# Attention in a two-layer decoder trunk: filling products four steps ahead, queries split over all rows and placed by transfers, weight splits half a chunk ahead and in pieces

## The chip, the cores and the metric

The kernel runs on one core of a Trainium2 chip. The metric is the device time of one execution in microseconds (us): three executions gave 931.06, 931.27 and 932.01, the median is 931.27. One more execution was taken with the hardware profiler; all rows with start times come from it. The engines of a core are PE (TensorE, matrix products, with PEld for its weight loads), DVE (VectorE), ACT (ScalarE), POOL (GpSimd) and SP (SyncE, which here only issues DMA transfers). Each runs its own instructions in order and waits for others by semaphores.

## The reference

Two layers over a sequence of 512 tokens with 1024 features. Layer 0 mixes tokens by causal pooling, layer 1 by attention; a gated MLP follows each, with a norm ahead of every part. The change touches only the attention of layer 1:

```python
qkv = h @ w_qkv + b_qkv                    # 16 query heads, 4 key/value heads of 64
kb, vb = band(k), band(v)                  # this block of 128 keys and the one before
scores = einsum("bnqkgd,bnskd->bnkgqs", q, kb) * 64 ** -0.5
scores = where(mask, scores - slope * dist, -inf)      # window of 128, ALiBi
m = maximum(max(scores), sink)
p = exp(scores - m)
probs = p / (sum(p) + exp(sink - m))
o = einsum("bnkgqs,bnskd->bnqkgd", probs, vb)
h = h + o @ w_o
```

## The kernel before, in words

**Products of float32.** A float32 number is held as a rounded high part (`_h`) and the rest (`_l`). `mm3` (L82 to L86) makes a product of three: wh·xh (L84), wh·xl (L85), wl·xh (L86). So every operand is split: a cast to the high part and a subtraction for the low part. "A product" below is one of the three matmuls, "a step" one call of `mm3` over 512 columns.

**Weights.** `fetch` (L88 to L91) has SP issue the transfer of 128x1024 numbers (512 KB) into a `raw` tile, of which there are 3. `weights` (L93 to L100) casts it on ACT (L98) and subtracts on DVE or POOL (L99), into rings of 4 `wh` and 4 `wl` tiles. A fetch waits until the split of the weight three earlier has read its `raw` tile, a cast until PE has done with the weight four earlier.

**Attention, set-up** (L382 to L493). Ten chunks of 128 output columns hold keys (`kq0`, `kq1`) and queries (`kq2` to `kq9`, called query chunks 0 to 7); a chunk is 8 steps. Keys, values and the first two query chunks are made ahead of the main loop. `keys(n)` (L440) splits 64 rows of a key head and puts the same into the other 64 rows (ACT L449, DVE L450). `queries(c)` (L453) multiplies the chunk by the norm's factor (DVE L456), scales it and adds the bias (ACT L457), and for each of its two heads casts 64 rows (ACT L463) and subtracts into the other 64 rows (DVE L464); a tile `q` thus has a head's high part in one half of the rows and its low part in the other.

**Main loop** (L601 to L620). There are 16 units: four key heads n by four blocks b of 128 queries. Unit i runs `scores` (8 matmuls L548 into a PSUM bank, masked and reduced by DVE L551, POOL L562, exp on ACT L565, sums on DVE L567 and L568, normalised by POOL L570). In the same turn, unit i−3 runs `weighted` (6 or 12 products with the values, then ACT L597 and DVE L598 split the result into `oh` and `ol`), and unit i−2 runs `transposed` (4 or 8 transposes on PE, L578, split by ACT L581 and DVE L582 into `th` and `tl`). Key heads n+1 are placed in the block b = 2 of head n.

**Filling products.** PE would idle between these. `work()` (L509) is one list of steps to fill with: 48 steps of query chunks 2 to 7, then steps of the output projection with weights `wo0` to `wo3`, each with the number of units that must be done ahead of it. `fill(upto, have)` takes steps up to a number, as long as their need is met. In turn i the loop takes 2/3 of `RATE` = 4 steps after the scores and the rest after the transposes, up to step 4i + 4. At the head of a new key head it takes at least the steps that the head's query chunks need. After the loop the rest is taken, then `wo0` to `wo7` are finished (L622 to L627).

The order of the code sets the work around the change; the framework (`tile.TileContext`, L767) then gives each engine a sequence of its own, close to the code's but not equal to it, in which SP's fetches and transfers stand about where their buffers or data are ready.

Of the kernel before, what the change touches and what calls it, by code (L numbers as in the profile page):

```python
# [19 lines left out]
F32 = mybir.dt.float32  # L20
F32R = mybir.dt.float32r
# [5 lines left out]
P = 128  # L27
# [30 lines left out]
def trunk(ctx: ExitStack, tc: tile.TileContext, x_tok, x_t, vecs, w_pool, w_kq, w_v, w_o, w_in, w_out, out_a, out_b):  # L58
# [10 lines left out]
    def small(pool, n, words, dt=F32, **kw):  # L69
        return pool.tile([P, words], dt, **kw)[:, :n]  # L70
# [19 lines left out]
        nc.sync.dma_start(raw[:, :n], src)  # L90
        return raw  # L91

    def weights(src, n, name, eng=None, raw=None):  # L93

        raw = raw or fetch(src, n, name)
        h = wp.tile([P, 1024], F32R, tag="wh", name=f"{name}_h")
        l = wp.tile([P, 1024], F32R, tag="wl", name=f"{name}_l")
        A.activation(h[:, :n], raw[:, :n], AF.Copy)  # L98
        (eng or V).tensor_tensor(l[:, :n], raw[:, :n], h[:, :n].bitcast(F32), ALU.subtract)  # L99
        return h, l  # L100

    def part(w, k, m=P):
# [280 lines left out]
    with tc.tile_pool(name="ap", bufs=2) as ap:  # L383
# [20 lines left out]
        nsink = small(ap, NH, 64, name="nsink", bufs=1)  # L404
        V.tensor_scalar(nsink, vec[:, V_SINK : V_SINK + NH], -1.0, None, ALU.mult)

        def proj(i, ps, ks=range(NC), w=None):
            w = w or weights(w_kq[i], D, f"kq{i}", G if i > 3 else V)
            for k in ks:
                mm3(ps, part(w, k), xs1[k], k == 0, k == NC - 1)  # L410
            return w
# [28 lines left out]
        def keys(n):  # L440

            src = slice((n % 2) * HD, (n % 2 + 1) * HD)
            dst = slice((1 - n % 2) * HD, (2 - n % 2) * HD)
            u = ku[n // 2]
            kh = ap.tile([P, S], F32R, tag="kh", name=f"kh{n}")
            kl = ap.tile([P, S], F32R, tag="kl", name=f"kl{n}")
            A.activation(kh[src], u[src], AF.Copy)
            V.tensor_tensor(kl[src], u[src], kh[src].bitcast(F32), ALU.subtract)
            A.activation(kh[dst], u[src], AF.Copy)  # L449
            V.tensor_copy(kl[dst], kl[src].bitcast(F32))  # L450
            return kh, kl

        def queries(c, ps):  # L453

            u = sm.tile([P, S], F32, tag="sq", name=f"q{c}_u")
            V.tensor_tensor(u, ps, rb, ALU.mult)  # L456
            A.activation(u, u, AF.Identity, scale=qs[:, c : c + 1], bias=bqs[:, c : c + 1])  # L457
            res = []
            for par in range(2):
                src = slice(par * HD, (par + 1) * HD)  # L460
                dst = slice((1 - par) * HD, (2 - par) * HD)
                t = ap.tile([P, S], F32R, tag="q", name=f"q{c}_{par}", bufs=8)
                A.activation(t[src], u[src], AF.Copy)  # L463
                V.tensor_tensor(t[dst], u[src], t[src].bitcast(F32), ALU.subtract)  # L464
                res.append(t)
            return res

# [1 line left out]
        q = {0: queries(0, qps)}  # L469
        qps = bank("pj")  # L470
        proj(3, qps)
        for j in range(NT):
            ps = vps[j // 2][:, (j % 2) * 256 : (j % 2 + 1) * 256]
            vv = ap.tile([P, 256], F32, tag="vv", name=f"vv{j}", bufs=1)
            V.scalar_tensor_tensor(vv, ps, r[:, j : j + 1], vec[:, V_BV : V_BV + 256], ALU.mult, ALU.add)
            dh, dl = (t[:, j, : 8 * HD].rearrange("p (n z d) -> p n z d", n=4, z=2)[:, :, 1, :] for t in (vh, vl))
            v4 = vv.rearrange("p (n d) -> p n d", n=4)
            A.activation(dh, v4, AF.Copy)
            V.tensor_tensor(dl, v4, dh.bitcast(F32), ALU.subtract)
# [7 lines left out]
        def fill_q(c):  # L487
            st = {}
            for k in range(NC):
                if k == 0:  # L490
                    st["ps"] = bank("pj")
                    st["w"] = None
                st["w"] = proj(2 + c, st["ps"], [k], st["w"])  # L493
                if k == NC - 1:
                    q[c] = queries(c, st["ps"])
                yield
# [5 lines left out]

        def fill_wo(m, tag, ks):
            if m not in wo_w:
                wo_w[m] = weights(w_o[m], D, f"wo{m}", G if m < 4 else V)
                wo_ps[m] = bank(tag)
            yield from wo_steps(m, ks)

# [19 lines left out]
        def fill(upto, have):  # L528
            while done[0] < upto and need[0] <= have:
                need[0] = next(todo, 100)  # L530
                done[0] += 1

        def scores(n, b):
            w = P if b == 0 else 2 * P
            neg = small(ap, 4, 32, tag="neg", name=f"neg{n}{b}", bufs=3)
            den = small(ap, 4, 16, tag="den", name=f"den{n}{b}", bufs=3)
            es = small(ap, 4, 16, tag="es", name=f"es{n}{b}", bufs=3)
            sink = nsink[:, 4 * n : 4 * n + 4]
            kk = max(b - 1, 0) * P
            sc = []  # L540
            for pr in range(2):
                ps = bank("s")
                st = ap.tile([P, 2, 2 * P], F32, tag="sc", name=f"sc{n}{b}{pr}", bufs=6)
                for par in range(2):
                    o = ps[:, par * 256 : par * 256 + 256]
                    qt = q[2 * n + pr][par][:, b * P : (b + 1) * P]
                    for x, kt in enumerate(key[n]):
                        T.matmul(o, lhsT=qt, rhs=kt[:, kk : kk + 256], start=x == 0, stop=x == 1)  # L548
                for par in range(2):
                    i = 2 * pr + par  # L550
                    V.tensor_tensor_reduce(  # L551
                        out=st[:, par, :w],
                        in0=ps[:, par * 256 : par * 256 + w],
                        in1=dist[:, 2 * P - w :],
                        scale=-slopes[4 * n + i],
                        scalar=sink[:, i : i + 1],
                        op0=ALU.add,
                        op1=ALU.min,
                        accum_out=neg[:, i : i + 1],
                    )  # L560
                sc.append(st)
            G.tensor_tensor(es, neg, sink, ALU.subtract)  # L562
            heads = [sc[i // 2][:, i % 2, :w] for i in range(4)]
            for i, t in enumerate(heads):
                A.activation(t, t, AF.Exp, bias=neg[:, i : i + 1], scale=-1.0, accum_out=den[:, i : i + 1])  # L565
            A.activation(es, es, AF.Exp)
            V.tensor_tensor(den, den, es, ALU.add)  # L567
            V.reciprocal(den, den)  # L568
            for i, t in enumerate(heads):
                G.tensor_scalar(t, t, den[:, i : i + 1], 1.0, ALU.mult, ALU.mult)  # L570
            return sc
# [26 lines left out]
            V.tensor_tensor(dl, p2, dh.bitcast(F32), ALU.subtract)  # L598


        RATE = 4  # L601
        sc, pt = {}, {}
        for i in range(NU + 3):
            base = i * RATE
            have = max(i - 3, 0) if i < NU else NU
            if i < NU:
                n, b = units[i]
# [164 lines left out]
```

## Time and profile before

| what | value |
|---|---|
| median of three executions | 931.27 us |
| the profiled execution | 932.39 us |
| its span, first to last instruction | 930.6 us |
| mean granted PE clock | 0.996 of full speed |
| data moved by DMA | 88.13 MB, 95 GB/s |

Columns of the timeline: start, duration, engine, line, operation, output<-inputs, shape, count; in brackets the idle time ahead of it and what ended it. Matmuls overlap, so the distance between starts tells what one costs, rather than its duration. A row of the waits has the waiting engine and line, what it waited for, then us in total, times, and the longest. A row of the groups has count, busy us, mean ns of one, idle us ahead.

### The profile page before, as it was taken

To read this page: it belongs to the slowest core of one execution; us is meant where nothing else is said; L and a number is where in the kernel's file an instruction comes from. 1 tells how busy PE (TensorE), PEld (TensorE's weight loads), DVE (VectorE), ACT (ScalarE), POOL (GpSimd) and SP (SyncE) were. 2 spreads that over 40 slices of the span, in tenths; PEclk is the share of its full clock that TensorE was granted. 3 is DMA by queue.
4 is the path that set the end of the run, shared out by engine and by line. 5 is a ranking of instruction groups with operands and counts; after the bars stand their busy time and mean duration, and the time that the engine had idled before them with its cause. 6 is when DMAs were issued, how large, how long until landed. Compare 5 with 4: busy or idle time off the path is not lost.

```text
span 930.6 us, 11682 instructions
## 1 busy us (share of the span) xinstructions
PE 915.2 (98%) x4419; PEld 771.5 (83%) x4419; DVE 574.8 (62%) x945; ACT 427.3 (46%) x690; POOL 135.1 (15%) x217
## 2 busy tenths in 40 slices
PE   8999999999999999999899999999999999999996
PEld 7788888888888888898788888888888888888896
DVE  5679766335777754456777482987743377777433
ACT  7655443223444443337787451644422244444532
POOL 9600000000000001325654140000000000000022
PEclk9999999999999999999999999999999999999999
DMA  9133222333223223322111041242233422322312
GB/s 333 67 113 113 93 84 80 93 128 113 91 91 105 65 87 106 114 91 68 50 43 46 2 158 39 98 139 104 63 93 100 136 91 91 111 80 63 95 60 91
DMA packets 28855, 88.13 MB, mean 95 GB/s; under 512 B 3200, under 2 KB 4352, under 8 KB 28800
## 3 DMA queue, kind: packets, MB, share of 16 engines
q1 hardware_dynamic: 28800, 87.40, 28.5%
q8 instruction: 34, 0.56, 0.2%
q14 instruction: 21, 0.17, 0.1%
HBM read 85.29 MB, written 2.10 MB: 94 GB/s over the span
## 4 chain that ended last, share of the span: by engine, by line
PE 92%; ACT 3%; DVE 2%; POOL 2%; issue 1%; POOLq 0%; ACTq 0%
PE bank L84 30%; PE bank L85 30%; PE bank L86 30%; PE bank L548 1%; PE bank L578 1%; ACT sc L565 1%; DVE q L464 1%; ACT px_h L251 0%; POOL sc L570 0%; PE bank L241 0%; ACT q_u L457 0%; DVE sc L551 0%; ACT wi_h L98 0%; PE bank L271 0%; ACT th L581 0%
## 5 line engine op out<-in xcount | busy, mean ns | idle before, releaser
L224 POOL TENSOR_TENSOR n_acc<-n_acc,n_sq 128x512 f32<-128x512 f32 (+1 forms) x28 | 39.1, 1395 | 716.4 <-ACT n_sq L215 709.8
L98 ACT ACTIVATE wi_h<-wi_raw 128x1024 fp32r<-128x1024 f32 x88 | 93.0, 1061 | 109.0 <-PE bank L85 100.5
L85 PE MATMUL bank<-f0x_l,wi_h 128*128 128x512 f32 x352 | 137.1, 389 | 0.8 <-DVE f0x_l L252 0.8
L84 PE MATMUL bank<-f0x_h,wi_h 128*128 128x512 f32 x352 | 137.3, 390 | 0.0
L84 PE MATMUL bank<-f1x_h,wi_h 128*128 128x512 f32 x352 | 137.2, 390 | 0.0
L84 PE MATMUL bank<-zh,wo_h 128*128 128x512 f32 (+1 forms) x363 | 137.1, 378 | 0.0
L86 PE MATMUL bank<-f0x_h,wi_l 128*128 128x512 f32 x352 | 137.0, 389 | 0.0
L86 PE MATMUL bank<-f1x_h,wi_l 128*128 128x512 f32 x352 | 137.0, 389 | 0.0
L85 PE MATMUL bank<-f1x_l,wi_h 128*128 128x512 f32 x352 | 137.0, 389 | 0.0
L86 PE MATMUL bank<-zh,wo_l 128*128 128x512 f32 (+1 forms) x363 | 136.6, 376 | 0.0
L85 PE MATMUL bank<-zl,wo_h 128*128 128x512 f32 (+1 forms) x363 | 136.6, 376 | 0.0
L99 DVE TENSOR_TENSOR wi_l<-wi_raw,wi_h 128x1024 fp32r<-128x1024 f32 x84 | 102.6, 1223 | 49.2 <-ACT wi_h L98 37.3
L98 ACT ACTIVATE wo_h<-wo_raw 128x768 fp32r<-128x768 f32 (+1 forms) x70 | 57.5, 823 | 120.2 <-PE bank L85 108.5
L313 DVE TENSOR_TENSOR c_u<-bank,n_rb 128x512 f32<-128x512 f32 x88 | 59.9, 687 | 75.9 <-PE bank L86 75.9
L99 DVE TENSOR_TENSOR wo_l<-wo_raw,wo_h 128x768 fp32r<-128x768 f32 (+1 forms) x66 | 60.3, 914 | 54.4 <-ACT wo_h L98 54.2
L86 PEld LDWEIGHTS bank<-zh,wo_l 128*128 128x128 f32 x363 | 68.3, 188 | 12.5
L84 PEld LDWEIGHTS bank<-zh,wo_h 128*128 128x128 f32 x363 | 68.3, 188 | 12.3
L85 PEld LDWEIGHTS bank<-zl,wo_h 128*128 128x128 f32 x363 | 68.3, 188 | 12.3
L85 PEld LDWEIGHTS bank<-f0x_l,wi_h 128*128 128x128 f32 x352 | 66.1, 188 | 14.6 <-DVE f0x_l L252 1.2
L84 PEld LDWEIGHTS bank<-f0x_h,wi_h 128*128 128x128 f32 x352 | 66.1, 188 | 14.2 <-DVE h L305 0.4
L86 PEld LDWEIGHTS bank<-f1x_h,wi_l 128*128 128x128 f32 x352 | 66.1, 188 | 13.9
L316 ACT ACTIVATE c_t<-c_u,vec 128x512 f32<-128x512 f32 x88 | 70.6, 811 | 15.3 <-DVE c_u L313 14.5
(173 smaller groups left out, 1488.7 us busy)
## 6 DMA issues: line engine op xcount, KB each, us to landing
wi_raw<-w_in SPq DMA_DIRECT2D x88, 512.0 KB, 3.2
wo_raw<-w_out SPq DMA_DIRECT2D x31, 384.0 KB, 3.0
wo_raw<-w_out SPq DMA_DIRECT2D x31, 320.0 KB, 2.8
kq_raw<-w_kq SPq DMA_DIRECT2D x10, 512.0 KB, 3.2
wo_raw<-w_o SPq DMA_DIRECT2D x8, 512.0 KB, 3.2
xt<-x_tok SPq DMA_DIRECT2D x4, 512.0 KB, 5.2
h<-x_t SPq DMA_DIRECT2D x8, 256.0 KB, 7.5
wpool_raw<-w_pool SPq DMA_DIRECT2D x2, 512.0 KB, 8.5
```

Of the source, the lines that this page charges most:

```text
L84: T.matmul(ps, lhsT=wh, rhs=xh, start=start, stop=False, **kw)
L85: T.matmul(ps, lhsT=wh, rhs=xl, start=False, stop=False, **kw)
L86: T.matmul(ps, lhsT=wl, rhs=xh, start=False, stop=stop, **kw)
L98: A.activation(h[:, :n], raw[:, :n], AF.Copy)
L99: (eng or V).tensor_tensor(l[:, :n], raw[:, :n], h[:, :n].bitcast(F32), ALU.subtract)
L224: eng.tensor_tensor(self.acc[:, lo:hi], self.acc[:, lo:hi], sq[:, lo:hi], ALU.add)
L313: V.tensor_tensor(u, ps, rb, ALU.mult)
L316: A.activation(t, u, AF.Identity, bias=col(V_CB + layer * 2 * NF + m), scale=cw[2])
L464: V.tensor_tensor(t[dst], u[src], t[src].bitcast(F32), ALU.subtract)
L548: T.matmul(o, lhsT=qt, rhs=kt[:, kk : kk + 256], start=x == 0, stop=x == 1)
L565: A.activation(t, t, AF.Exp, bias=neg[:, i : i + 1], scale=-1.0, accum_out=den[:, i : i + 1])
L578: T.transpose(ps[:, i * P : (i + 1) * P], sc[i // 2][:, i % 2, kb * P : (kb + 1) * P], ident)
```

## The change

- `AHEAD` = 4: four filling steps are taken ahead of the first unit, and every limit in the loop is four steps higher.
- A query chunk is split over all 128 rows at once: one cast into a tile `qh`, one subtraction in place. The halves are then put into the `q` tiles by four transfers (`move`, each 64x512 numbers, 128 KB), issued by SP.
- The copies of the keys into the other 64 rows become two such transfers.
- The weights of a query chunk are asked for half a chunk ahead (at k = 4 of the chunk before) and not at its first step. From `kq5` on their subtraction is on POOL in four pieces of 256 columns, as is that of `wo0` to `wo3`; that of `kq4` moves from POOL to DVE.
- `vv` uses the ring `sc`, and `neg`, `den` and `es` have 2 buffers where they had 3.

```diff
-    def weights(src, n, name, eng=None, raw=None):
+    def weights(src, n, name, eng=None, raw=None, step=1024):
...
-        (eng or V).tensor_tensor(l[:, :n], raw[:, :n], h[:, :n].bitcast(F32), ALU.subtract)
+        for a in range(0, n, step):
+            o = slice(a, min(a + step, n))
+            (eng or V).tensor_tensor(l[:, o], raw[:, o], h[:, o].bitcast(F32), ALU.subtract)
...
+        def query_weights(i):
+            return weights(w_kq[i], D, f"kq{i}", G if i > 4 else V, step=256 if i > 4 else 1024)
+
+        def move(dst, src):
+            nc.sync.dma_start(dst.bitcast(F32), src.bitcast(F32))
+
         def proj(i, ps, ks=range(NC), w=None):
-            w = w or weights(w_kq[i], D, f"kq{i}", G if i > 3 else V)
+            w = w or query_weights(i)
...
-            A.activation(kh[dst], u[src], AF.Copy)
-            V.tensor_copy(kl[dst], kl[src].bitcast(F32))
+            move(kh[dst], kh[src])
+            move(kl[dst], kl[src])
...
+            th = ap.tile([P, S], F32R, tag="qh", name=f"q{c}_h", bufs=1)
+            tl = u.bitcast(F32R)
+            A.activation(th, u, AF.Copy)
+            V.tensor_tensor(tl, u, th.bitcast(F32), ALU.subtract)
...
-                A.activation(t[src], u[src], AF.Copy)
-                V.tensor_tensor(t[dst], u[src], t[src].bitcast(F32), ALU.subtract)
+                move(t[src], th[src])
+                move(t[dst], tl[src])
...
+        next_w = [query_weights(4)]
...
-            vv = ap.tile([P, 256], F32, tag="vv", name=f"vv{j}", bufs=1)
+            vv = ap.tile([P, 256], F32, tag="sc", name=f"vv{j}", bufs=6)
...
-                    st["w"] = None
-                st["w"] = proj(2 + c, st["ps"], [k], st["w"])
+                    st["w"] = next_w.pop()
+                proj(2 + c, st["ps"], [k], st["w"])
+                if k == NC // 2 and c < NC - 1:
+                    next_w.append(query_weights(3 + c))
...
-                wo_w[m] = weights(w_o[m], D, f"wo{m}", G if m < 4 else V)
+                wo_w[m] = weights(w_o[m], D, f"wo{m}", G if m < 4 else V, step=256 if m < 4 else 1024)
...
-        RATE = 4
+        RATE, AHEAD = 4, 4
         sc, pt = {}, {}
+        fill(AHEAD, 0)
         for i in range(NU + 3):
-            base = i * RATE
+            base = AHEAD + i * RATE
```

**SP, the last fetches of the attention.** Before, SP's sequence here is fetches alone (`wo0` to `wo7` are the output projection's weights, `wi1_…` those of the MLP):

```order
L90 DMA wo3_raw_4563<-w_o 128x1024
L90 DMA wo4_raw_4656<-w_o 128x1024
L90 DMA wo5_raw_4694<-w_o 128x1024
L90 DMA wo6_raw_4732<-w_o 128x1024
L90 DMA wo7_raw_4770<-w_o 128x1024
L90 DMA wi1_0_1_raw_4812<-w_in 128x1024
```

Now (`q6_0`, `q6_1` are the tiles of the two heads of query chunk 6, `q6_h` its high part, `q6_u` the low part; `kl3` is the low part of key head 3):

```order
L413 DMA kl3_4144<-kl3_4144 64x512
L90 DMA wo5_raw_4745<-w_o 128x1024
L413 DMA q6_0_4037<-q6_h_4034 64x512
L413 DMA q6_0_4037<-q6_u_4031 64x512
L413 DMA q6_1_4040<-q6_h_4034 64x512
L413 DMA q6_1_4040<-q6_u_4031 64x512
L90 DMA wo6_raw_4783<-w_o 128x1024
L413 DMA q7_0_4189<-q7_h_4186 64x512
L413 DMA q7_0_4189<-q7_u_4183 64x512
L413 DMA q7_1_4192<-q7_h_4186 64x512
L413 DMA q7_1_4192<-q7_u_4183 64x512
L90 DMA wo7_raw_4821<-w_o 128x1024
```

The transfers of a chunk stand between fetches. Those of chunk 7 follow the fetch of `wo6`; in the same way those of chunk 1 follow the fetch of `wo0`, and those of chunk 5 the fetch of `wo4`.

**PE, the turn of unit 14 (key head 3, block 2).** Ahead of these rows stand the weighted products of unit 10, and the transposes of unit 11 (`sc230`, `sc231`, whose split gives `th230` and so on). Before:

```order
L578 MATMUL bank6_76<-ident_104,sc231_4145 128x128 x2
L84 MATMUL bank0_70<-oh_3363,wo1_h_4317 128x512
L85 MATMUL bank0_70<-ol_3364,wo1_h_4317 128x512
L86 MATMUL bank0_70<-oh_3363,wo1_l_4318 128x512
L548 MATMUL bank3_73<-kh3_4089,q6_0_4054 128x256
L548 MATMUL bank3_73<-kl3_4090,q6_0_4054 128x256
L548 MATMUL bank3_73<-kh3_4089,q6_1_4057 128x256
L548 MATMUL bank3_73<-kl3_4090,q6_1_4057 128x256
```

Four more scores follow there (`q7_0`, `q7_1`), and then six products with `wo1`, ahead of the weighted products of unit 11. Now:

```order
L593 MATMUL bank6_76<-ident_104,sc231_4205 128x128 x2
L563 MATMUL bank3_73<-kh3_4143,q6_0_4037 128x256
L563 MATMUL bank3_73<-kl3_4144,q6_0_4037 128x256
L563 MATMUL bank3_73<-kh3_4143,q6_1_4040 128x256
L563 MATMUL bank3_73<-kl3_4144,q6_1_4040 128x256
L563 MATMUL bank4_74<-kh3_4143,q7_0_4189 128x256
L563 MATMUL bank4_74<-kl3_4144,q7_0_4189 128x256
L563 MATMUL bank4_74<-kh3_4143,q7_1_4192 128x256
L563 MATMUL bank4_74<-kl3_4144,q7_1_4192 128x256
L84 MATMUL bank1_71<-th230_4396,vh_3050 128x256
L85 MATMUL bank1_71<-tl230_4397,vh_3050 128x256
```

The nine products with `wo1` are gone from this place: the fill is four steps ahead and the next steps still need a unit that isn't done.

**PE, the end of the loop.** `th331` is the last unit's transposed block. Before:

```order
L86 MATMUL bank1_71<-th331_4559,vl_3051 128x256
L84 MATMUL bank2_72<-oh_3363,wo3_h_4565 128x512
L85 MATMUL bank2_72<-ol_3364,wo3_h_4565 128x512
L86 MATMUL bank2_72<-oh_3363,wo3_l_4566 128x512
L84 MATMUL bank2_72<-oh_3363,wo3_h_4565 128x512
L85 MATMUL bank2_72<-ol_3364,wo3_h_4565 128x512
```

Four more products with `wo3` follow, then those of `wo0`. Now:

```order
L86 MATMUL bank1_71<-th331_4625,vl_3051 128x256
L84 MATMUL bank5_75<-oh_3375,wo0_h_4226 128x512
L84 MATMUL bank0_70<-oh_3375,wo1_h_4300 128x512
L84 MATMUL bank4_74<-oh_3375,wo2_h_4526 128x512
L85 MATMUL bank5_75<-ol_3376,wo0_h_4226 128x512
L86 MATMUL bank5_75<-oh_3375,wo0_l_4227 128x512
L84 MATMUL bank5_75<-oh_3375,wo0_h_4226 128x512
```

The products with `wo3` that stood here are taken earlier, and the products behind the last unit now need its `oh` and `ol` at once.

More of the change, by code (lines that the diff above doesn't have):

```diff
@@ L534, in scores @@
             w = P if b == 0 else 2 * P
-            neg = small(ap, 4, 32, tag="neg", name=f"neg{n}{b}", bufs=3)
-            den = small(ap, 4, 16, tag="den", name=f"den{n}{b}", bufs=3)
-            es = small(ap, 4, 16, tag="es", name=f"es{n}{b}", bufs=3)
+            neg = small(ap, 4, 32, tag="neg", name=f"neg{n}{b}")
+            den = small(ap, 4, 16, tag="den", name=f"den{n}{b}")
+            es = small(ap, 4, 16, tag="es", name=f"es{n}{b}")
             sink = nsink[:, 4 * n : 4 * n + 4]
```

## Prediction

> **What bounds the kernel now.** I read the page's busy table first, then what TensorE (PE) waits for, over the whole run.
>
> ```profile
> PE 915.2 (98%) x4419; PEld 771.5 (83%) x4419; DVE 574.8 (62%) x945; ACT 427.3 (46%) x690; POOL 135.1 (15%) x217
> PE bank L548 <- DVE q L464: 3.4, 2, 2.9
> ```
>
> PE is busy for 98% of the span, so only what PE loses counts. In attention the second row tells of two waits of the scores (L548) for the queries' low half (L464). The PE timeline shows them with their idle time in brackets, and one wait more, of the weighted values for `tl`.
>
> ```profile
> 441.05 0.39 PE L85 MATMUL bank<-tl,vh 128*128 128x256 f32 x1 [0.44 <-DVE tl L582]
> 451.64 0.38 PE L548 MATMUL bank<-kh,q 128*128 128x256 f32 x1 [2.86 <-DVE q L464]
> 455.80 0.40 PE L84 MATMUL bank<-ax_h,kq_h 128*128 128x512 f32 x1
> 475.86 0.39 PE L548 MATMUL bank<-kh,q 128*128 128x256 f32 x1 [0.58 <-DVE q L464]
> ```
>
> Why L464 was late stands on POOL and DVE.
>
> ```profile
> 446.34 4.70 POOL L99 TENSOR_TENSOR kq_l<-kq_raw,kq_h 128x1024 fp32r<-128x1024 f32 x2 [0.19 <-ACT kq_h L98]
> 448.85 3.45 DVE L464 TENSOR_TENSOR q<-q_u,q 64x512 fp32r<-64x512 f32 x2 [2.09 <-ACT q L463]
> ```
>
> Two weight splits run on POOL until 451.04. DVE's two L464 take 3.45 us together and end only after POOL's split does; I read this as DVE standing still while POOL works. And the wait costs more than its 2.86 us: the clock that PE was granted, in windows of 3.41 us.
>
> The columns are length, PE busy, instructions, granted clock, DMA share, GB/s.
>
> ```profile
> 448.79:452.20 3.41, 0.56 (x3) 1.00 0.52 165
> 452.20:455.61 3.41, 3.41 (x14) 0.50 0.39 143
> 472.68:476.09 3.41, 2.83 (x20) 1.00 0.00 0
> 923.24:926.65 3.41, 0.72 (x6) 1.00 0.46 164
> 926.65:930.07 3.42, 0.00 (x0) 0.50 0.71 274
> ```
>
> Behind windows with 0.56 and 0.72 us of work, the next one has half the clock. The window with the 0.58 us wait in it (2.83 busy) does no harm: at 475.86 the scores run at their usual pace. So somewhere between 0.72 and 2.83 us of work in such a window it is decided.
>
> **The change part by part.** Unit prices on PE come from one undisturbed stretch.
>
> ```profile
> 503.06 0.28 PE L84 MATMUL bank<-th,vh 128*128 128x256 f32 x1
> ...
> 504.50 1.04 PE L578 MATMUL bank<-ident,sc 128*128 128x128 f32 x8
> 505.29 0.47 PE L84 MATMUL bank<-oh,wo_h 128*128 128x512 f32 x1
> 505.60 0.39 PE L85 MATMUL bank<-ol,wo_h 128*128 128x512 f32 x1
> ...
> 506.06 0.28 PE L548 MATMUL bank<-kh,q 128*128 128x256 f32 x1
> ...
> 507.01 0.40 PE L84 MATMUL bank<-oh,wo_h 128*128 128x512 f32 x1
> ```
>
> From start to start: 12 weighted products 1.44, 8 transposes 0.79, three products behind transposes 0.77, a product otherwise 0.23 (two from 505.60 to 506.06), 8 scores 0.95.
>
> *Gains.* The scores between 451.64 and 455.80 are 12 (0.12 each, 1.43) with 4 products (0.23 each, 0.92): 2.35 at full clock, and 4.16 was used, so the half clock cost 1.8. Pieces of a quarter bound the stop of DVE by one piece, and the fill that runs four steps ahead changes which work stands between a chunk's end and its first use. Taken away: 2.86 + 1.8 + 0.58 + 0.44 = 5.7 us. The 0.44 has new neighbours in the order and I count it whole.
>
> *Pieces on POOL.* No row has a 128x256 split; the nearest are these.
>
> ```profile
> L224 POOL TENSOR_TENSOR n_acc<-n_acc,n_sq 128x256 f32<-128x256 f32 x3 | 2.2, 737 | 8.8 <-ACT n_sq L215 8.8
> L99 POOL TENSOR_TENSOR wo_l<-wo_raw,wo_h 128x1024 fp32r<-128x1024 f32 x4 | 9.6, 2405 | 2.2 <-ACT wo_h L98 2.2
> ```
>
> Four pieces cost between 2.4 and 2.95; I take 2.95. DVE may step in between them, 0 to 0.7 (one instruction of DVE's 0.68 below); I take 0.4. By itself that is off PE's path. It is not any more because of what follows.
>
> *The transfers.* Each chunk's queries now end in four transfers of 128 KB issued by SP. SP issues in order, and its order puts the transfers of chunks 1, 5 and 7 behind the fetches of `wo0`, `wo4` and `wo6`, which wait until POOL has ended the split that frees their `raw` buffer (`kq7_l`, `wo1_l`, `wo3_l`). The splits' casts wait in turn for the end of the same chunk, since PE reads the ring's oldest weights until then. For a transfer from SBUF to SBUF there is no row; the nearest are an output of the same 128 KB and a weight fetch, with the fetch's landing times in 380 to 440.
>
> ```profile
> out_a<-o SPq DMA_DIRECT2D x8, 128.0 KB, 1.7
> L681 SPq DMA_DIRECT2D out_a<-o x8: 332/332/348, 919.1 to 924.2; - x8
> kq_raw<-w_kq SPq DMA_DIRECT2D x10, 512.0 KB, 3.2
> DMA to landing us min/median/max: 3.1/3.4/4.4
> ```
>
> Behind a 512 KB fetch, a transfer lands at worst after it: 3.2 and 0.3 for each further 128 KB (the second of two fetches landed 1.2 later, a quarter of that), so 3.8 from the fetch's issue for the two that one head needs. At best it lands 1.7 after its own issue: 3 issues of 0.33 and 1.7, 2.7. I take 3.8: both use the same queue. The Trainium skill ("DMA: Bandwidth & Descriptors", "Anatomy of one DMA — SWDGE (gpsimd) path") gives a fixed 2.0 us and bytes at 436 GB/s, an estimate of 2.3 us for 128 KB; the 1.7 of the row is shorter, and by the page the sum would have 0.6 more at chunk 3.
>
> *When they are needed.* Ends of chunks, and the cast and the query steps behind them:
>
> ```profile
> 425.42 0.28 PE L548 MATMUL bank<-kh,q 128*128 128x256 f32 x1
> 425.39 1.06 ACT L98 ACTIVATE kq_h<-kq_raw 128x1024 fp32r<-128x1024 f32 x1 [1.88 <-PE bank L85]
> 471.05 0.28 PE L548 MATMUL bank<-kh,q 128*128 128x256 f32 x1
> 472.86 2.41 POOL L99 TENSOR_TENSOR wo_l<-wo_raw,wo_h 128x1024 fp32r<-128x1024 f32 x1
> 494.97 0.28 PE L548 MATMUL bank<-kh,q 128*128 128x256 f32 x1
> 495.02 1.05 ACT L98 ACTIVATE wo_h<-wo_raw 128x1024 fp32r<-128x1024 f32 x1
> 495.87 0.68 DVE L456 TENSOR_TENSOR q_u<-bank,n_rb 128x512 f32<-128x512 f32 x1
> 496.59 0.82 ACT L457 ACTIVATE q_u<-q_u,bqs,qs 128x512 f32<-128x512 f32 x1 [0.51 <-DVE q_u L456]
> ```
>
> Each L548 here is the first PE instruction behind a chunk, so its start is the chunk's end (T).
>
> - Chunk 1: cast to 426.45, pieces and DVE 3.35: fetch at 429.8, queries at 433.6. The new order has 26 products and 8 scores between: 26 × 0.23 + 0.95, needed at T + 6.9 = 432.4. Wait 1.2 (0.1 to 1.6).
> - Chunk 3 has no fetch just ahead: L457 ends at T + 2.4, one copy of about 0.8 and some queue, one subtraction of 0.7, two issues and 1.7: T + 6.3 to 7.2, needed at T + 6.7. Wait 0.2 (0 to 0.5).
> - Chunk 5: POOL starts between T + 1.1 (as at chunk 7) and T + 1.8 (as in the row of 472.86): queries at T + 8.3 to 9.0. In the new order stand between: 8 scores, 9 products, 6 weighted products, 8 transposes, 3 products, 4 scores, 7 products: 0.95 + 2.07 + 0.72 + 0.79 + 0.77 + 0.48 + 1.61, needed at T + 7.4. Wait 1.3 (0.3 to 2.3).
> - Chunk 7: cast to T + 1.1, pieces 3.35, transfers 3.8: T + 8.3. Between stand 12 scores, 15 products (3 behind 8 transposes) and 9 weighted products: 0.95 + 1.38 + 0.72 + 0.79 + 0.77 + 0.48 + 1.38 + 0.36, needed at T + 6.8. Wait 1.5 (0.4 to 1.8).
>
> *Holes that running ahead opens.* Four steps taken earlier are missing later: at unit 11 the weighted products now follow the transposes with only 8 scores between, at the end the output products need the last unit at once.
>
> ```profile
> 505.88 1.29 DVE L582 TENSOR_TENSOR tl<-bank,th 128x512 fp32r<-128x512 f32 x2
> 528.11 0.40 PE L84 MATMUL bank<-oh,wo_h 128*128 128x512 f32 x1
> 528.31 0.39 ACT L597 ACTIVATE oh<-bank 128x256 fp32r<-128x256 f32 x1 [2.85 <-PE bank L86]
> 528.73 0.43 DVE L598 TENSOR_TENSOR ol<-bank,oh 128x256 fp32r<-128x256 f32 x1 [2.43 <-ACT oh L597]
> ```
>
> The first `tl` is there at 506.5, 1.25 after the transposes' end at 505.29; 0.95 covers it: 0.3 (0.2 to 0.5). `oh` is ready at 528.70, 0.6 after the last weighted product (0.5 to 0.9); `ol` at 529.16 is covered by the three products that need `oh` alone.
>
> *Nothing:* the keys' transfers stand two units ahead of their use, some 12 us (the four units between the ends of chunks 5 and 7 take 23.9). The split of `kq4` on DVE lies beside a whole projection of PE (24 × 0.23 = 5.5 us).
>
> ```profile
> L99 DVE TENSOR_TENSOR kq_l<-kq_raw,kq_h 128x1024 fp32r<-128x1024 f32 x4 | 4.9, 1224 | 5.2 <-ACT kq_h L98 5.2
> ```
>
> Without that cover it costs 1.2 at most. The shallower rings of `neg`, `den` and `es`, a ring shared by `vv`, and casts half a chunk earlier find DVE, ACT and POOL with the spare share of the first row; gone, each would be a wait of one instruction, 0.4 to 1.1.
>
> *Sum.* New waits 1.2 + 0.2 + 1.3 + 1.5 + 0.3 + 0.6 = 5.1 against 5.7: 0.6 less. The profiled execution took 932.39 (span 930.6 and 1.8 around it), 1.1 above the median of 931.27; taken off the median: 930.7.
>
> **The rivals.**
>
> *The transfers overtake the fetch's bytes.* Spread over 16 engines, a small one may land 1.7 after its issue. Then the waits are 0.1, 0.2, 0.3, 0.4, 0.3 and 0.6, 1.9 together, the gain 3.8: 927.5. For it: in 448.79 to 452.20 the DMA share is only 0.52 while fetches run. Against: the second of two fetches landed 1.2 later than the first.
>
> *A half clock comes back, slower.* If chunk 5's or 7's queries come 2.7 us late rather than 1.3 or 1.5, a window is left with under 0.72 us of work, and the next runs at half the clock. The place is the first scores from chunk 5 or 7, the price 1.4 more wait and 1.8 of clock: −0.6 + 3.2 = +2.6, 933.9; both, about 937. It decides between 0.58, which did no harm, and 2.86, which did. For it: four transfers behind POOL and a fetch give three places to be late; against: my waits are about half as long.
>
> *The dip was not the wait's.* The row shows half clock right behind the window with 0.56 us of work. If it was set off by something else and stays, the gain is 1.8 less: +1.2, 932.5. The Trainium skill ("TensorE: Matmul & The Clock Gate", "HAM oscillation — how this bites in real kernels") says that gaps of PE up to about 3.4 us are harmless; the 2.86 us wait then would not have done it. The rows of 452.20 and 926.65 speak against that.
>
> **How the numbers follow.** Forecast 0.47, overtaking 0.33, half clock 0.15, dip that stays 0.05. About 0.2% (1.9 us) is what a measurement of this kernel can tell from no change. Faster: all of overtaking and 0.03 of the forecast's own spread (DVE takes no time from POOL, 1.2; chunk 3 and the holes at their low ends, 0.4: waits of 3.5, 929.1), 0.36. Slower: half clock, and 0.05 of the forecast (waits at their high ends, 7.6, give 933.2), 0.20. The rest, 0.44, is the same. The forecast's own range is 929.1 to 933.2; to hold 8 in 10 it reaches to overtaking at 927.5 and to one half clock at 933.9.
>
> **What would show it.** Right: no wait of PE for POOL or for a subtraction where 451.64 stands now, no half clock near it; in its place PE waits for transfers at the first scores from chunks 1, 5 and 7, each 0.8 to 1.8 us, with SP's own wait for POOL's last piece ahead of them; 0.6 at the last unit. Wrong: transfers that land within 2 us of their issue behind a fetch; a window at half clock; a wait over 2.7 us; PE waiting for weights, keys or `neg`.

## The result, and the profile after

The changed kernel took 940.69 us (median of 4, 939.79 to 941.05), the kernel before 931.16 beside it (931.03 to 932.01): 1.0095 of the time, 95% interval 1.0083 to 1.0108. So it is slower by about 9 us, where no measurable change was forecast, and it lies outside the forecast's range (927.5 to 933.9).

One thing must be known of the kernel before: of its 66 executions taken alongside the experiments, 15 took 930.8 to 931.2 with a mean clock of 0.998, and 51 took 931.7 to 933.7 with 0.995 to 0.997. The profiled one (932.39, clock 0.996) is of the larger group, and the medians 931.27 and 931.16 are of the smaller. The ratios of the experiments are against runs of the kernel before taken beside them; the median of those was 932.2 to 932.5. Against these, the 940.69 would be 1.009.

In the page of the kernel after, PE's busy time has grown by 2.6 us and its idle time by 5.8:

```profile
PE 917.8 (98%) x4419; PEld 774.3 (82%) x4419; DVE 566.7 (60%) x934; ACT 418.7 (45%) x678; POOL 137.9 (15%) x243
```

Its waits of PE (waiting line, what it waited for, total, times, longest; L563 is L548 of before, L596 and L597 are L581 and L582, L612 is L597, L101 is L99; L468 and L469 are the new cast and subtraction of the queries; in the kernels of the experiments the lines shift by a few more):

```profile
PE bank L563 <- DMA q<-q_u: 9.5, 4, 3.2
...
PE bank L84 <- ACT oh L612: 0.5, 1, 0.5
...
PE bank L85 <- DVE tl L597: 0.3, 1, 0.3
PE bank L84 <- ACT th L596: 0.2, 1, 0.2
```

No wait for a subtraction (L464 before) is left, as forecast; but the scores now wait four times for the transfer of a low part. The timeline of PE has these waits in brackets; its first row is the first instruction of PE behind chunk 1, whose start is the chunk's end:

```profile
426.06 0.39 PE L84 MATMUL bank<-ax_h,kq_h 128*128 128x512 f32 x1
...
436.32 0.36 PE L563 MATMUL bank<-kh,q 128*128 128x256 f32 x1 [3.21 <-DMA q<-q_u]
...
451.77 0.36 PE L563 MATMUL bank<-kh,q 128*128 128x256 f32 x1 [1.10 <-DMA q<-q_u]
...
479.59 0.55 PE L563 MATMUL bank<-kh,q 128*128 128x256 f32 x1 [3.03 <-DMA q<-q_u]
...
505.75 0.36 PE L563 MATMUL bank<-kh,q 128*128 128x256 f32 x1 [2.16 <-DMA q<-q_u]
```

The four rows with a wait are the first scores of chunks 1, 3, 5 and 7. In windows of 3.41 us (length, PE busy and instructions, granted clock, DMA share, GB/s), the waits at chunks 5 and 7 are followed by half clock, the one at chunk 1 is not:

```profile
475.69:479.10 3.41, 0.87 (x4) 1.00 0.92 266
479.10:482.52 3.42, 2.93 (x12) 0.50 0.08 20
503.00:506.41 3.41, 1.25 (x9) 1.00 0.65 196
506.41:509.82 3.41, 3.41 (x19) 0.50 0.02 5
431.32:434.73 3.41, 1.78 (x10) 1.00 0.93 254
434.73:438.14 3.41, 1.82 (x10) 1.00 0.61 165
```

Work at half clock takes twice as long, so half of the 2.93 and the 3.41 us of busy time there is lost: 3.2 us. The account for the span is +9.5 for the waits for transfers, +3.2 for the half clock and +1.0 for the waits for `th`, `tl` and `oh`, against the 2.9, 1.8, 0.6 and 0.4 of before that are gone: +8.0, where the span grew by 8.4 (930.6 to 939.0). The other 0.4 is one wait outside attention (for `rs_y`, 1.6 before and 2.0 now).

Chunk 1 shows why the transfers are late. These are POOL's pieces, SP's issues, and the landing of the four transfers, which is the time from an issue until its data are there (the view of the line that issues them, from 430 to 437):

```profile
427.18 3.31 POOL L101 TENSOR_TENSOR kq_l<-kq_raw,kq_h 128x256 fp32r<-128x256 f32 x4 [0.68 <-ACT kq_h L98]
```

```profile
430.52 0.33 SPq L90 DMA_DIRECT2D wo_raw<-w_o  x1
430.94 0.47 SPq L413 DMA_DIRECT2D q<-q_h  x1
431.52 0.52 SPq L413 DMA_DIRECT2D q<-q_u  x1
```

```profile
DMA to landing us min/median/max: 4.2/4.6/4.7
```

The pieces end at 430.49 and the fetch of `wo0` goes at 430.52, both within 0.2 us of the forecast's working. The first head's low part goes 1.0 us after the fetch, where two issues of 0.33 would make 0.7. But the scores that need it start only at 436.32. At chunk 3, with no fetch just ahead (448 to 453), the same view says:

```profile
DMA to landing us min/median/max: 2.2/2.3/2.3
```

Two windows show the engines that carry them, first with the fetch and four transfers, then with four transfers alone (DMA share and GB/s are the last two columns):

```profile
432.00:435.00 3.00, 1.10 (x7) 1.00 1.00 277
449.75:452.50 2.75, 1.65 (x9) 1.00 0.81 190
```

In the first the 16 DMA engines are full. In the second, four transfers of 128 KB keep them busy for 0.81 of 2.75 us, which is 0.56 us of all the engines for each (an estimate from this row), not 0.3.

The fetches show the other side. This is the landing of the seven fetches of `wo0` to `wo6` in the kernel before, then that of the fetches after the change, from 428 to 506 (the line L90 in both):

```profile
DMA to landing us min/median/max: 3.1/3.2/3.3
```

```profile
DMA to landing us min/median/max: 3.2/3.9/4.7
```

After the change, the fetches with no transfer right behind them (issued at 435.91 and 452.31) still land after 3.2 us. The other five, with four transfers right behind, take 3.8 to 4.7; those of `wo0`, `wo4` and `wo6` are 4.5, 4.7 and 3.9.

### The profile page after: what moved, and what is told of

It reads as the page before. It is cut to its first block, busy times and chain, and to the rows that moved or that the text cites. A ratio compares the mean times of both kernels' runs of the same rounds, so it can differ in the third digit from the quotient of the medians.

```text
span 939.0 us, 11777 instructions
## 1 busy us (share of the span) xinstructions
PE 917.8 (98%) x4419; PEld 774.3 (82%) x4419; DVE 566.7 (60%) x934; ACT 418.7 (45%) x678; POOL 137.9 (15%) x243
## 4 chain that ended last, share of the span: by engine, by line
PE 49%; POOL 1%; DMA 1%; ACT 1%; DVE 0%; issue 0%; POOLq 0%; DVEq 0%; ACTq 0%
PE bank L85 15%; PE bank L84 15%; PE bank L86 15%; PE bank L593 1%; PE bank L563 1%; DMA q<-q_u 1%; POOL sc L585 0%; POOL wo_l L101 0%; POOL kq_l L101 0%; ACT sc L580 0%; DVE ob L724 0%; PE bank L243 0%; PE bank L671 0%; PE bank L232 0%; POOL es L577 0%
## 5 line engine op out<-in xcount | busy, mean ns | idle before, releaser
L101 DVE TENSOR_TENSOR wi_l<-wi_raw,wi_h 128x1024 fp32r<-128x1024 f32 x84 | 102.5, 1223 | 49.4 <-ACT wi_h L98 37.6
L101 DVE TENSOR_TENSOR wo_l<-wo_raw,wo_h 128x768 fp32r<-128x768 f32 (+1 forms) x66 | 60.9, 924 | 54.6 <-ACT wo_h L98 54.4
```

What stands on the lines that cost most here:

```text
L101: (eng or V).tensor_tensor(l[:, o], raw[:, o], h[:, o].bitcast(F32), ALU.subtract)
```

## The experiments

Two theories stood against each other. By theory 1 the queries' transfers make the loss, either because they lie behind a fetch (1a: because of its bytes, 1a1, or of its wait for POOL, 1a2) or because of their own time (1b). By the rival, filling ahead and the pieces make it, and the transfers only show it.

**The transfers undone.** In the changed kernel:

```diff
-            th = ap.tile([P, S], F32R, tag="qh", name=f"q{c}_h", bufs=1)
-            tl = u.bitcast(F32R)
-            A.activation(th, u, AF.Copy)
-            V.tensor_tensor(tl, u, th.bitcast(F32), ALU.subtract)
...
-                move(t[src], th[src])
-                move(t[dst], tl[src])
+                A.activation(t[src], u[src], AF.Copy)
+                V.tensor_tensor(t[dst], u[src], t[src].bitcast(F32), ALU.subtract)
```

> The changed kernel with one part undone: the queries are split and placed by ACT and DVE as before the change; filling four steps ahead, the pieces, the earlier weights and the keys' transfers stay. Theory 1 (the queries' transfers make the loss: 9.5 us of waits and two stretches of half clock of about 1.5 us each): these 12.5 us go, a wait for a subtraction of up to 0.7 may come, so 928 to 929. Rival (filling ahead and the pieces make the loss, the transfers only show it): 936 or more, with the waits put down to another instruction.

928.76 us, 0.9963 of before (0.9950 to 0.9976). The loss is gone, and what remains of the change is a gain of 3.5 us on the median beside it. Theory 1 holds, and the 928 to 929 expected came. PE's waits in this kernel:

```profile
PE bank L559 <- DVE q L472: 1.9, 3, 1.3
...
PE bank L84 <- ACT oh L608: 0.5, 1, 0.5
```

**The transfers alone.** In the kernel before, the reverse of the edit above (with `move` and the rings).

> The kernel before with one part of the change alone: queries split over all rows and placed by transfers; weights in one piece, at the chunk's first step, nothing filled ahead (vv, neg, den and es use the rings of the change, since qh needs the space). Before, a chunk's queries are needed about 4.2 us after its end (chunk 5: end 471.05, wait from 475.28). Theory 1: they come 7.9 (no fetch ahead, as chunk 3 after the change) to 10 us (fetch ahead) after it, so waits of 4 to 6 us at four chunks, with half clock behind each: 948 to 955. Rival (transfers are harmless without filling ahead): 930 to 933.

940.75 us, 1.0092 (1.0076 to 1.0107): the time of the whole change (940.69), from the transfers alone. The waits for them are 8.0 us in three places, and two windows at half clock follow:

```profile
PE bank L555 <- DMA q<-q_u: 8.0, 3, 3.6
```

The 948 to 955 expected was too much, since the order moved with the edit: chunk 5 ends there at 469.79 and its first scores are due at 476.88, 7.1 us later, where it was 4.2 before. So this expectation failed on the size, and the two runs agree on the cause: without the transfers the loss goes, and with them alone it comes.

**The transfers on ACT.** One word in the changed kernel:

```diff
-            nc.sync.dma_start(dst.bitcast(F32), src.bitcast(F32))
+            nc.scalar.dma_start(dst.bitcast(F32), src.bitcast(F32))
```

> The changed kernel with the transfers issued by ACT and not by SP, so that none stands behind a fetch that waits for POOL. Theory 1a (standing behind the fetch is most of the loss): transfers start as soon as the split is done and land 2.3 us after their issue, waits of about 1.1 at each of four chunks as at chunk 3, no half clock: 940.7 - 5.1 - 3 = 932 to 933, up to 1 more for the issues on ACT. Theory 1b (the time of a transfer itself is most of it): waits stay near 2 to 3 at three chunks: 938 or more.

941.86 us, 1.0106 (1.0088 to 1.0124). By the time alone, 1b would have it. The waits say otherwise:

```profile
PE bank L563 <- DMA q<-q_u: 2.4, 3, 1.2
PE bank L86 <- POOL wo_l L101: 2.3, 2, 1.3
PE bank L84 <- ACT th L596: 2.0, 2, 1.8
...
PE bank L84 <- DVE ol L613: 1.7, 2, 1.4
PE bank L86 <- POOL kq_l L101: 1.4, 1, 1.4
```

The scores' waits for transfers fall from 9.5 to 2.4 us and the median landing of all these transfers from 3.7 to 2.4, which fits 1a; but each issue holds ACT (a row of that kernel's view has 16 of them at 0.47 to 2.0 us, median 0.61), and PE now waits for `th`, for weights and for `ol`, with one window at half clock. So the run moved the loss to another place and did not measure 1a. One of its transfers tells something more: ACT issued it at 429.81, 0.13 us ahead of SP's fetch of 429.94, and it landed only after 4.3 us. So in this one case a fetch delayed a transfer that stood in another queue and was issued first. The page of this kernel gives that queue a row of its own (packets, MB, share of the span of 940.3 us on all 16 engines):

```profile
q10 hardware_dynamic: 3200, 5.25, 2.4%
```

These are 40 transfers of 128 KB, so each takes 0.56 us of all the engines, as in the window above.

**Small fetches ahead of the transfers.** In the changed kernel, for m = 0, 4 and 6 (it leaves out all but 16 of the 1024 columns of these weights, so that its output is not the reference's and only its time counts):

```diff
+            raw = fetch(w_o[m][:, :16], 16, f"wo{m}")
...
+            v = vh.rearrange("p a b -> p (a b)")[:, :1024].bitcast(F32)
+            A.activation(h, v, AF.Copy)
+            eng.tensor_tensor(l[:, :16], raw[:, :16], h[:, :16].bitcast(F32), ALU.subtract)
```

> The changed kernel, but the fetches of wo0, wo4 and wo6 bring 16 of 1024 columns, and their casts and subtractions read another tile for the rest: so the wait for POOL ahead of the transfers stays, and the 512 KB ahead of them go. Theory 1a1 (the bytes on the shared engines delay the transfers): landing falls from 3.6 to 4.8 to 2.3 us, waits at chunks 1, 5 and 7 fall from 3.2, 3.0 and 2.2 to about 1.0, 1.0 and 0.4, no half clock: about 932.5. Theory 1a2 (the wait for POOL and the issue are the delay): waits stay at 2 to 3, about 940.

936.38 us, 1.0045 (1.0029 to 1.0061). PE's timeline:

```profile
433.33 0.36 PE L579 MATMUL bank<-kh,q 128*128 128x256 f32 x1 [1.77 <-DMA q<-q_u]
...
454.18 0.55 PE L579 MATMUL bank<-kh,q 128*128 128x256 f32 x1 [4.90 <-DMA q<-q_u]
...
479.84 0.36 PE L579 MATMUL bank<-kh,q 128*128 128x256 f32 x1 [1.02 <-DVE neg L582]
...
502.90 0.35 PE L579 MATMUL bank<-kh,q 128*128 128x256 f32 x1 [0.71 <-DMA q<-q_u]
```

At chunks 1, 5 and 7 the waits fall from 3.21, 3.03 and 2.16 (8.4 together) to 1.77, 1.02 and 0.71 (3.5). (The releaser named at 479.84 is the last by the profile; that the row is the first scores of chunk 5, waiting for their transfer, is my reading.) The landings show the bytes' part without the change of order: behind the small fetches the transfers of these chunks land 2.2 to 2.4 us after their issue, as alone, where behind whole fetches it was 3.6 to 4.8. So 1a1 holds for the larger part: the 512 KB ahead cost each transfer some 1.3 to 2.5 us. The 4.9 us by which the waits fell are not this alone, since the scores moved too (chunk 1's first are due 6.1 us behind its end, and not 7.1). The time did not fall to 932.5, because in this order chunk 3's transfers came to stand behind the whole fetch of `wo2`, landed after 3.8 to 4.4 us, and made a wait of 4.90 with a window at half clock behind it: the same cause at another place.

**One part at a time.** Pieces alone, and filling ahead alone, each in the kernel before:

```diff
-            w = w or weights(w_kq[i], D, f"kq{i}", G if i > 3 else V)
+            w = w or weights(w_kq[i], D, f"kq{i}", G if i > 3 else V, step=256 if i > 3 else 1024)
```

> The kernel before with one part alone: the subtractions on POOL (kq4 to kq9, wo0 to wo3) in four pieces of 256 columns. If DVE stands still while POOL works on a piece, the wait of 2.86 before the change shrinks to one or two pieces' length at most (0.7 to 1.4), the half clock behind it (1.8) goes, and 0.58 shrinks too: gain 3.3 to 4.5, so 927 to 928. Rival (DVE was late for ACT, not for POOL): nothing changes, 931.

```diff
-        RATE = 4
+        RATE, AHEAD = 4, 4
+        fill(AHEAD, 0)
...
-            base = i * RATE
+            base = AHEAD + i * RATE
```

> The kernel before with one part alone: filling four steps ahead. If what counts is the distance from a chunk's end to its first use, the four steps (12 x 0.23 = 2.8 us) cover the wait of 2.86, no half clock follows, 0.58 goes, and the two holes of 0.5 each come (as after the change): 931.2 - 2.8 - 1.8 - 0.6 + 1.0 = 927. Rival (running ahead only moves the hole): 931 or more, with waits for th, tl or oh in place of those for q.

929.99 us, 0.9977 (0.9968 to 0.9986), and 929.96 us, 0.9979 (0.9970 to 0.9988). Each gains some 2.5 us on the median beside it; 3.3 to 4.5 was expected, to 927 or 928, so both expectations were too good. Against the executions of before without half clock (930.8 to 931.2), each gains about 1. The waits of the first, then of the second:

```profile
PE bank L550 <- DVE q L466: 2.8, 4, 1.0
```

```profile
PE bank L548 <- DVE q L464: 2.3, 3, 1.3
```

The long wait is broken up (longest 1.0 and 1.3), and neither has a window at half clock in attention in its profiled execution; but 2 to 3 us of short waits stay.

**Eight steps ahead.** In the changed kernel `AHEAD = 8`.

> The changed kernel with AHEAD = 8 in place of 4. If the loss is that transfers land later than the scores need them, four more steps give 2.8 us more: waits of 3.2, 1.1, 3.0 and 2.2 become 0.4, 0, 0.2 and 0, the half clock goes (12 less in all), and the holes at unit 11 and the end grow by 1 to 3: 930 to 932. Rival (the transfers hold up more than the first scores): 937 or more.

933.84 us, 1.0015 (1.0006 to 1.0024): 7 less than with four steps, 2 more than the 930 to 932 expected. Chunks 3, 5 and 7 wait for transfers no more, chunk 1 does, and half clock follows there:

```profile
435.17 0.55 PE L563 MATMUL bank<-kh,q 128*128 128x256 f32 x1 [3.15 <-DMA q<-q_u]
```

Chunk 1's first scores did not move back against its end: they are due 7.0 us behind it, as with four steps. That the framework puts them where it expects the transfer to be done is my reading and was not tried. More distance removes the wait where the order gives it.

**Pieces and early weights, no transfers, nothing ahead.** The kernel with the transfers undone, `AHEAD = 0`, the keys' transfers undone too.

> The changed kernel without any transfer inside the chip (queries and keys placed by ACT and DVE as before) and with AHEAD = 0: so pieces, kq4 on DVE and weights asked for half a chunk ahead remain. If early weights add nothing, it is as the kernel with pieces alone, 927 to 928; against the kernel with the queries' transfers undone (928.8) the difference tells what running ahead is worth: lower if its two holes cost more than its cover brings.

930.17 us, 0.9981 (0.9972 to 0.9990). That is the time of pieces alone (929.99): early weights add nothing that can be seen. The same kernel with four steps ahead has 0.9961 (the run without any transfers, below); so running ahead is worth about 0.2% there, though the intervals overlap a little.

**POOL taken out.** The kernel with the queries' transfers undone, and:

```diff
-            return weights(w_kq[i], D, f"kq{i}", G if i > 4 else V, step=256 if i > 4 else 1024)
+            return weights(w_kq[i], D, f"kq{i}", V, step=1024)
...
-                wo_w[m] = weights(w_o[m], D, f"wo{m}", G if m < 4 else V, step=256 if m < 4 else 1024)
+                wo_w[m] = weights(w_o[m], D, f"wo{m}", V, step=1024)
```

> The kernel with the queries' transfers undone (e1), and all the attention's weight subtractions on DVE in one piece, none on POOL. In e1 the two L472 at 445.12 took 3.30 us and ended with POOL's four pieces. If DVE stands still for POOL's subtractions, the pair takes 1.2 to 1.6 again, the waits of 1.27, 0.42 and 0.22 go, and PE gains 1.5 on e1: 0.995 of before, or 927.2 where before is 931.2. Rival (the pair is long for another reason, or DVE's own splits, 1.2 us each, delay the queries as much): as e1 or longer, 0.9963 or more.

926.07 us, 0.9932 (0.9919 to 0.9946): faster than the kernel before and than the one with the transfers undone, and 1 us below what was expected. In the kernel with the transfers undone, DVE's pair and POOL's four pieces stood so:

```profile
445.12 3.30 DVE L472 TENSOR_TENSOR q<-q_u,q 64x512 fp32r<-64x512 f32 x2
```

```profile
444.31 2.81 POOL L101 TENSOR_TENSOR kq_l<-kq_raw,kq_h 128x256 fp32r<-128x256 f32 x4
```

And now DVE's pair, with no split of POOL beside it:

```profile
444.03 1.43 DVE L472 TENSOR_TENSOR q<-q_u,q 64x512 fp32r<-64x512 f32 x2
```

No wait of PE for queries is left in attention; its one wait there is the 0.5 for the last `oh`. DVE stood still for POOL, and cutting POOL's work into pieces did not free it at this place.

**Six steps ahead.** The kernel with the queries' transfers undone, `AHEAD = 6`.

> The kernel with the queries' transfers undone (e1), with AHEAD = 6 in place of 4. By distance: two more steps are 1.4 us more, the wait of 1.27 goes and 0.42 too where the order moves with it; the holes at unit 11 and at the end grow by up to 1. Against e1 0.5 to 1.7 faster: 0.9945 to 0.996 of before. Rival (the holes take it all): 0.9963 or more.

931.69 us, 0.9994 (0.9986 to 1.0003): the rival holds, and two more steps ahead cost 3 us. The waits for queries go and others come:

```profile
PE bank L84 <- DVE ol L609: 2.1, 2, 1.4
PE bank L85 <- DVE tl L593: 1.6, 6, 0.5
```

**No transfers at all.** The queries' and the keys' transfers undone, four steps ahead.

> The kernel with the queries' transfers undone (e1), and the keys' transfers undone too (copies on ACT and DVE as before). If the keys' transfers cost nothing, as the prediction says, the time is that of e1: 0.995 to 0.9975 of before. If they save DVE and ACT time on the path, it is over 0.9975.

928.61 us, 0.9961 (0.9949 to 0.9974): as expected, and as with the keys' transfers kept (0.9963): these cost nothing that can be measured.

**Only the splits on DVE.** In the kernel before, `G if i > 3 else V` and `G if m < 4 else V` become `V`.

> The kernel before with one edit: all the attention's weight subtractions on DVE in one piece (kq4 to kq9 and wo0 to wo3 were on POOL); nothing ahead, no transfers. If POOL's subtractions held DVE's L464, and that made the waits of 2.86 and 0.58 (with half clock in some executions), these go, DVE has 10 x 1.2 us more to do, and the time comes to 927 to 928.5 where before is 931.2, a ratio of 0.9955 to 0.997. If running ahead is needed besides (e9, 0.9932), waits for q of 0.5 to 1 stay at the chunk ends. Rival (DVE gets too full): 0.998 or more.

927.87 us, 0.9953 (0.9940 to 0.9967), as expected: more than any part of the change gave alone. Waits for queries of 1.0 us in two places are left, which do not stand in the run above with four steps ahead.

## Why the prediction was wrong

**The step that failed** is the landing of a transfer behind a fetch, "3.8 from the fetch's issue for the two that one head needs". The scores that need the two started 5.8, 5.9 and 5.2 us after it at chunks 1, 5 and 7 (430.52 to 436.32, 473.69 to 479.59, 500.58 to 505.75; the last two fetches' issues stand in SP's timeline):

```profile
473.69 0.33 SPq L90 DMA_DIRECT2D wo_raw<-w_o  x1
...
500.58 0.33 SPq L90 DMA_DIRECT2D wo_raw<-w_o  x1
```

Both terms of the 3.8 were too small. The fetch itself was taken at 3.2, but with four transfers right behind it on the same engines it landed after 4.5, 4.7 and 3.9 (3.2 without them). Each transfer was taken at 0.3 more, and landed 0.5 to 0.7 behind the fetch or transfer ahead of it. The 0.3 came from a misread row: of the two fetches in 380 to 440 that go 1.2 us apart, the first landed 3.7 and the second 4.4 us after its own issue, so 1.9 apart, and 1.2 is only what the second took beyond 3.2. A quarter of 1.9 is 0.5.

A row for the same bytes on another route (an output, 1.7) was taken for the price at chunk 3; alone it was 2.2 to 2.3. The estimate of 2.3 that the prediction took from the Trainium skill and left out of its sum came close there; the section that it names is on transfers that GpSimd issues, while SP issues these, so this does not test it. And an issue took 0.46 to 0.63, not 0.33. My range for the landing, 2.7 to 3.8, had its upper end as the value; a range should have had a price for full engines above it.

So the waits for transfers came to 9.5 where the sum has 4.2, and two of them set off a half clock of 3.2 that the sum left out. With the 1.8 of a gain that was not there (below), this is about the whole distance from 930.7 to 940.69.

**What held.** The fetch goes 4.5 us after the end of chunk 1 (forecast 4.4), the four pieces ahead of the transfers of chunks 1, 5 and 7 take 3.31, 3.28 and 2.84 (forecast 3.35, DVE's steps included), and the scores are due 7.1, 6.9, 7.5 and 7.1 us behind chunks 1, 3, 5 and 7 (forecast 6.9, 6.7, 7.4 and 6.8). The last hole is 0.5 (0.6). The hole at unit 11 did not show; 0.5 stood instead behind chunk 3's wait. So the mechanism was right for chunks 1, 5 and 7: their transfers come late, behind a fetch that waits for POOL, and show as waits of PE. Its price was wrong.

**Chunk 3** waited 1.10, not 0.2. The landing made 0.5 of it, ACT most of the rest: the scaling that ended 2.4 us behind the chunk at chunk 7 of before ended 3.9 behind it here. ACT's rows (chunk 3 ends at 443.81) show a wait for POOL, then the cast of the next weights, which began 2.1 behind the chunk and not 0.05, and then the scaling:

```profile
445.33 0.20 ACT L581 ACTIVATE es<-es 128x4 f32<-128x4 f32 x1 [0.92 <-POOL es L577]
...
445.92 1.05 ACT L98 ACTIVATE kq_h<-kq_raw 128x1024 fp32r<-128x1024 f32 x1
446.87 0.81 ACT L465 ACTIVATE q_u<-q_u,bqs,qs 128x512 f32<-128x512 f32 x1
```

**The rival of the half clock** was given 0.15 and 933.9 to 937, and is what happened, twice, with 3.2 us together. The time is above even the 937 for both, since chunk 1 waited 3.21 us and not 1.2 as well. The half clock came at a wait of 2.16, below the 2.7 that I set; what decides is not the wait's length (last section). The other two rivals did not come: every transfer behind a fetch landed after it, so none overtook it, and half clock came behind windows short of work and nowhere else in attention.

**The gain** was overstated. The profiled execution had the half clock, and the clocks say that only part of the executions have it: one such window lowers the mean clock by 1.7 in 930 us, 0.002, which is the distance between 0.998 and 0.996. Taking its 1.8 off the median, which stood in the group without it, counted a gain that was not in it. The reading that DVE stands still for POOL is right, since without POOL's subtractions the pair takes 1.43 and the waits go. The claim that pieces bound the stop by one piece is not: beside four pieces the pair still took 3.30. In the kernel with pieces alone it took 2.00 where it was 3.45, so pieces help at times; when they do is open. The waits of 2.9, 0.6 and 0.4 did go.

**What stays open.** Without the fetches' bytes, 3.5 us of waits are left at chunks 1, 5 and 7. How much of this is the wait for POOL and how much the transfer's own 2.3 was not tried alone. At chunk 1 the low part was ready at 429.2, by the row below, and issued at 431.52; at chunks 5 and 7 it was ready 0.5 after the fetch's issue (474.2 and 501.1). So the fetch's wait for POOL can have mattered much only at chunk 1.

```profile
428.50 0.69 DVE L469 TENSOR_TENSOR q_u<-q_u,q_h 128x512 fp32r<-128x512 f32 x1 [1.55 <-ACT q_h L468]
```

## What to carry to other kernels

A step moved from a compute engine to a transfer is late by its issue, its landing and the bytes that share the engines with it; price the landing with the engines full, and look at what the queue's order puts next to it. When a price is read from two transfers in flight, take the time between their landings. Where PE waits for an engine that stands still beside another, first take the other's work away, before adding distance or pieces: here that one edit gained 4.5 us, and the whole change lost about 9. And where executions of a kernel differ by a window at half clock, say which kind the profiled one is before its time is set against a median.

## What the runs showed of the hardware

In the attention of these kernels, half clock follows a window with little work, and not a wait of some length. The windows' edges lie elsewhere in each execution: the half clock begins at 452.20 before and at 479.10 and 506.41 after, which fits one grid of 3.41 us within the second execution, but not one for both. A wait of 3.21 us divided between two windows (1.78 and 1.82 busy) did no harm, one of 2.16 us in one window (1.25 busy) did.

The other traces narrow the limit. On each execution's own grid, the 14 kept traces have 429 windows that begin between 425 and 530 us; eight have less than 1.6 us of work, and exactly these eight are followed by one window at half clock. The two nearest to the limit are these, in the kernel with the transfers on ACT and in the one with small fetches:

```profile
492.60:496.01 3.41, 1.58 (x12) 1.00 0.33 77
496.02:499.43 3.41, 3.01 (x15) 0.50 0.45 105
```

```profile
430.25:433.66 3.41, 1.64 (x9) 1.00 0.60 136
433.67:437.08 3.41, 3.41 (x22) 1.00 0.31 90
```

So the limit lies at about 1.6 us of busy time for the products of attention. It is not one for busy time of any kind: near the end of the run, where PE's last rows multiply by only 2 columns, a window with 2.40 us (925.19 to 928.60 in the kernel with small fetches) is followed by half clock too.

That the grid falls differently in each execution would explain the two groups of the kernel before, 930.8 to 931.2 at 0.998 and some 1.4 us more at about 0.996: its wait of 2.86 us would leave one window short of work in some executions and not in others. This is the likeliest reading, and wasn't tried. The Trainium skill ("TensorE: Matmul & The Clock Gate", "HAM oscillation — how this bites in real kernels") has gaps of more than about 3.4 us as what costs the clock; here 2.16 us was enough.

A DVE subtraction with both inputs in SBUF stands still while POOL subtracts, and DVE's reductions of the scores out of PSUM go on beside it. The pair of 64x512 took 3.45 and 3.30 us beside POOL's splits and 1.43 without them. In the kernel after, the same shows beside POOL's pieces:

```profile
470.39 3.28 POOL L101 TENSOR_TENSOR wo_l<-wo_raw,wo_h 128x256 fp32r<-128x256 f32 x4
...
470.43 0.48 DVE L566 CUSTOM_DVE_ANT_0 sc<-bank,dist,nsink 128x256 f32<-128x256 f32 x1
...
473.10 1.11 DVE L469 TENSOR_TENSOR q_u<-q_u,q_h 128x512 fp32r<-128x512 f32 x1
```

The reduction takes its usual 0.48; the subtraction takes 1.11 where it is 0.69 alone, and ends 0.54 after POOL's last piece. It does not always stand still for the whole of POOL's work: beside eight pieces in the kernel with pieces alone, the pair took 2.00 and ended before they did.
